# Instance norm on one core: ten middle units loaded in 64 KB rows into pairs of slots, each stored in two column halves

## The chip, the cores and the metric

The kernel runs on one NeuronCore of a Trainium2 chip. A core has a matrix engine (TensorE, PE in the profile), a vector engine (VectorE, DVE), an activation engine (ScalarE, ACT), a general engine (GpSimd, POOL) and SyncE (SP), which here only issues transfers. Sixteen DMA engines, shared by everything the core transfers, carry data between HBM and the on-chip memory of 128 partitions. A transfer issued by SP goes into the ring that the profile calls q1, one issued by ACT into q10, one issued by POOL into q0; each of the sixteen DMA engines has its own piece of each ring.

The metric is device time in microseconds, median over runs. Before the change it is 626.96 us (three runs, 626.79 to 627.2).

## The reference

```python
# x: (4, 8, 16, 256, 256) float32, gamma: (8, 16) float32
mu = x.mean(axis=(3, 4), keepdims=True)
var = ((x - mu) ** 2).mean(axis=(3, 4), keepdims=True)
x_norm = (x - mu) / np.sqrt(var + 1e-5)
out = x_norm * gamma[None, :, :, None, None]
```

There are 4 x 8 x 16 = 512 channels of 65,536 values. Each is normalized by its own mean and variance and multiplied by its gamma (128 different ones). Input and output are 134.2 MB each, and each value is read once and written once.

## The kernel before

**Units.** The 512 channels are cut into 32 units of 16 channels. A channel is spread over S = 8 partitions, 8,192 values (32 KB) in each, so that a unit is a tile of 128 partitions x 8,192 float32 (4 MB), contiguous in HBM. Six such tiles (`slots`, named xt in the profile) hold the units in flight; unit u lives in slot u mod 6.

**One unit.** Its load is issued by SP (L48; units 1 and 3 by ACT). VectorE sums each partition row (L107) while ScalarE squares and sums it (L108), writing the squares to a tile that nobody reads. TensorE multiplies the two columns of sums by a block matrix of -1/65536 (`navg`, L116), which adds up the eight partitions of each channel and hands the negative mean and the negative mean square back to all eight. A chain of small steps on VectorE and ScalarE makes the factor gamma/std (L117 to L127). VectorE then rewrites the tile in place, (x - mean) * scale (L130), and ACT issues its store (L134). At the end of the unit's turn SP is given the load of unit u + 6 (L136), which waits until the store of unit u has landed, since it writes into the same slot.

**Order.** The schedule is written by hand (`manual_schedule`): every engine runs its instructions in the program's order. ACT's queue holds, for each unit, the squares, the root and the issue of the store; the squares of unit u + 1 stand behind the issue of store u, which waits for L130. SP's queue holds only loads, in order.

**Setup.** A 0.5 KB load of gamma goes through POOL (L55). VectorE copies it out eight times (`g_rep`, L83), eight small matmuls turn it into one column per unit of a batch (L88), and a copy brings the columns on chip (`g_col`, L94). POOL builds `navg` (L67 to L72). Ahead of it all, a store of sixteen rows of 512 B of zeros goes to the place of unit 0's output (`touch`, L53 and L54; unit 0's own store overwrites it later and waits for it). The source also has sixty `nop` instructions on ScalarE (L60), which the order of the built program's instructions does not show.

Of the kernel before, what the change touches and what calls it, by code (L numbers as in the profile page):

```python
# [1 line left out]

# [4 lines left out]

F32 = mybir.dt.float32
U8 = mybir.dt.uint8
ALU = mybir.AluOpType  # L10
ACTF = mybir.ActivationFunctionType
AX = mybir.AxisListType


@with_exitstack
def kernel(
    ctx: ExitStack,
    tc: tile.TileContext,
    x: bass.AP,
    gamma: bass.AP,  # L20
    out: bass.AP,
):
    nc = tc.nc
    B, G, C, H, W = x.shape
    P = nc.NUM_PARTITIONS
    HW = H * W
    n_ch = B * G * C
    S = 8
    K = P // S
    F = HW // S  # L30
    U = n_ch // K
    NG = (G * C) // K
    AHEAD = 6
    assert HW % S == 0 and (G * C) % K == 0

    xv = x.rearrange("b g c h w -> (b g c h w)").rearrange("(u p f) -> u p f", p=P, f=F)
    ov = out.rearrange("b g c h w -> (b g c h w)").rearrange("(u p f) -> u p f", p=P, f=F)
    gv = gamma.rearrange("g c -> (g c)")

    data = ctx.enter_context(tc.tile_pool(name="data", bufs=1))  # L40
    singles = ctx.enter_context(tc.tile_pool(name="singles", bufs=1))
    psum = ctx.enter_context(tc.tile_pool(name="psum", bufs=4, space=bass.MemoryType.PSUM))
    ctx.enter_context(tc.manual_schedule())

    slots = [data.tile([P, F], F32, name=f"xt{i}") for i in range(AHEAD)]

    def load(u, queue):
        queue.dma_start(out=slots[u % AHEAD][:], in_=xv[u])  # L48


    g_row = singles.tile([1, G * C], F32, name="g_row")
    touch = singles.tile([16, 128], F32, name="touch")
    nc.vector.memset(touch[:], 0.0)  # L53
    nc.gpsimd.dma_start(out=ov[0][0::S, 0:128], in_=touch[:])  # L54
    nc.gpsimd.dma_start(out=g_row[:], in_=gv[None, :])  # L55
    for u in range(AHEAD):
        load(u, nc.scalar if u in (1, 3) else nc.sync)

    for _ in range(60):
        nc.scalar.nop()  # L60

    eps_t = singles.tile([P, 1], F32, name="eps_t")
    nc.gpsimd.memset(eps_t[:], 1e-5)
    one = singles.tile([1, 1], F32, name="one")
    nc.gpsimd.memset(one[:], 1.0)
    navg = singles.tile([P, K, S], F32, name="navg")
    nc.gpsimd.memset(navg[:], -1.0 / HW)  # L67
    nc.gpsimd.affine_select(  # L68
        out=navg[:], in_=navg[:], pattern=[[-S, K], [0, S]], compare_op=ALU.is_ge,
        fill=0.0, base=0, channel_multiplier=1,  # L70
    )
    nc.gpsimd.affine_select(  # L72
        out=navg[:], in_=navg[:], pattern=[[S, K], [0, S]], compare_op=ALU.is_ge,
        fill=0.0, base=S - 1, channel_multiplier=-1,
    )
    navg_w = navg[:].rearrange("p k s -> p (k s)")
    root_eps = singles.tile([P, 1], F32, name="root_eps")
    nc.scalar.activation(out=root_eps[:], in_=eps_t[:], func=ACTF.Sqrt)  # L78
    g_rep = singles.tile([1, NG, K, S], F32, name="g_rep")
    g_ps = psum.tile([P, NG], F32, name="g_ps", bufs=1)  # L80
    g_col = singles.tile([P, NG], F32, name="g_col")

    nc.vector.tensor_copy(  # L83
        out=g_rep[:],
        in_=g_row[:].rearrange("o (n k) -> o n k", n=NG).unsqueeze(3).to_broadcast([1, NG, K, S]),
    )
    for n in range(NG):
        nc.tensor.matmul(  # L88
            out=g_ps[:, n : n + 1],
            lhsT=g_rep[:, n].rearrange("o k s -> o (k s)"),  # L90
            rhs=one[:],
            start=True, stop=True,
        )
    nc.vector.tensor_copy(out=g_col[:], in_=g_ps[:])  # L94

    junk = singles.tile([P, F], U8, name="junk")

    st = singles.tile([P, U, 2], F32, name="st")
    nvar = singles.tile([P, U], F32, name="nvar")
    std = singles.tile([P, U], F32, name="std")  # L100
    rstd = singles.tile([P, U], F32, name="rstd")
    scale = singles.tile([P, U], F32, name="scale")

    squares = []
    for u in range(U):
        t = slots[u % AHEAD]
        nc.vector.reduce_sum(out=st[:, u, 0:1], in_=t[:], axis=AX.X)  # L107
        square = nc.scalar.activation(  # L108
            out=junk[:], in_=t[:], func=ACTF.Square, accum_out=st[:, u, 1:2],
        )  # L110
        if u:

            tc.declare_no_dep(square.ins, squares[-1].ins, reason="junk, ordered by the root between")
        squares.append(square)
        ps = psum.tile([P, 2], F32, name="ps")
        nc.tensor.matmul(out=ps[:], lhsT=navg_w, rhs=st[:, u], start=True, stop=True)  # L116
        nc.vector.tensor_scalar(  # L117
            out=nvar[:, u : u + 1], in0=ps[:, 0:1], scalar1=ps[:, 0:1],
            scalar2=ps[:, 1:2], op0=ALU.mult, op1=ALU.add,
        )  # L120
        nc.scalar.activation(  # L121
            out=std[:, u : u + 1], in_=nvar[:, u : u + 1], func=ACTF.Sqrt,
            bias=eps_t[:], scale=-1.0,
        )
        nc.vector.reciprocal(out=rstd[:, u : u + 1], in_=std[:, u : u + 1])  # L125
        g = u % NG
        nc.vector.tensor_mul(  # L127
            out=scale[:, u : u + 1], in0=rstd[:, u : u + 1], in1=g_col[:, g : g + 1],
        )
        nc.vector.tensor_scalar(  # L130
            out=t[:], in0=t[:], scalar1=ps[:, 0:1], scalar2=scale[:, u : u + 1],
            op0=ALU.add, op1=ALU.mult,
        )
        nc.scalar.dma_start(out=ov[u], in_=t[:])  # L134
        if u + AHEAD < U:
            load(u + AHEAD, nc.sync)  # L136


# [1 line left out]
_INS = ['x', 'gamma']  # L140
_OUTS = [((4, 8, 16, 256, 256), 'float32')]


# [23 lines left out]
```

## Time and profile before

| | |
|---|---|
| median of three runs | 626.96 us |
| profiled execution, first to last instruction | 624.9 us |
| HBM read and written | 134.22 MB and 134.23 MB |
| VectorE busy | 443.4 us (71%) |
| ScalarE busy | 238.8 us (38%) |
| TensorE, matmuls | 21.4 us (3%) |
| stores, ACT ring, issue to landing | 62.5 us median of 32 |
| loads, SP ring, issue to landing | 38.5 us median of 30 |

The profile's page gives the span of one profiled execution; what lies outside the span is the difference to the measured time. A transfer is cut into packets, one for each row here, and each packet is carried by one DMA engine. The trace records each packet's start, length and size, and this document uses these records beside the page. In the records a packet of 32,768 B takes 1,213 ns, one of 512 B takes 27 ns, and the 4 B packets with which each DMA engine reports the end of its share of a transfer take 9 ns.

### The profile page before, as it was taken

The page shows a single profiled execution, that of the slowest core. Times are in us where ns is not written, and L with a number is a line of the kernel's source. Part 1 is how long each engine was busy: PE and PEld are TensorE (multiplying, and loading weights), DVE is VectorE, ACT ScalarE, POOL GpSimd, SP SyncE. Part 2 cuts the span into 40 slices and gives each one's busy share as a digit, 9 for nine tenths or more (in the row PEclk, how much of TensorE's full clock was granted, in tenths as well). Part 3 has the DMA queues.
Part 4 walks back from the last instruction along what each step waited for, and adds up shares of the span by engine and source line. Part 5 has one row for each costly group of instructions (what it writes and reads, how often), then busy time and mean ns, then how long its engine had stood idle before and what let it go on. Part 6 is the DMA issues. An engine that isn't in the chain of part 4 may idle for free.

```text
span 624.9 us, 631 instructions
## 1 busy us (share of the span) xinstructions
PE 21.4 (3%) x80; PEld 19.5 (3%) x80; DVE 443.4 (71%) x163; ACT 238.8 (38%) x98; POOL 2.4 (0%) x11
## 2 busy tenths in 40 slices
PE   0200000000000000000000000000000000000000
PEld 0200000000000000000000000000000000000000
DVE  0588999999776687666786767867668676687730
ACT  0444444444443234432344423444224442244400
POOL 1000000000000000000000000000000000000000
DMA  8999999999999999999999999999999999999998
GB/s 370 436 426 430 422 434 436 436 436 437 432 424 433 436 436 424 436 436 434 436 436 432 422 436 436 434 426 436 436 434 436 436 434 419 436 436 434 426 436 369
DMA packets 9282, 268.46 MB, mean 430 GB/s; under 512 B 1072, under 2 KB 1088, under 8 KB 1088
## 3 DMA queue, kind: packets, MB, share of 16 engines
q10 hardware_dynamic: 4896, 142.61, 52.9%
q1 hardware_dynamic: 4320, 125.83, 46.8%
q0 software_dynamic: 64, 0.01, 0.0%
q14 instruction: 2, 0.02, 0.0%
HBM read 134.22 MB, written 134.23 MB: 430 GB/s over the span
## 4 chain that ended last, share of the span: by engine, by line
another core or an unknown queue 61%; DMA 17%; DVE 15%; SPq 1%; PE 1%; issue 0%; ACT 0%
DVE st L107 10%; DMA xt<-in_x_dram 10%; DMA out_dram<-xt 8%; DVE xt L130 5%; SPq L48 1%; PE ps L116 1%; ACT std L121 0%; DVE nvar L117 0%; DVE rstd L125 0%; DVE scale L127 0%
## 5 line engine op out<-in xcount | busy, mean ns | idle before, releaser
L107 DVE TENSOR_REDUCE st<-xt 128x1 f32<-128x8192 f32 x32 | 277.9, 8685 | 100.4 <-DMA xt<-in_x_dram 100.4
L108 ACT ACTIVATE junk<-xt 128x8192 uint8<-128x8192 f32 x32 | 225.0, 7030 | 275.1 <-DMA xt<-in_x_dram 231.9
L130 DVE TENSOR_SCALAR xt<-xt,ps,scale 128x8192 f32<-128x8192 f32 x32 | 145.6, 4550 | 1.2
L121 ACT ACTIVATE std<-nvar,eps_t 128x1 f32<-128x1 f32 x32 | 9.4, 294 | 79.6 <-DVE nvar L117 79.6
L116 PE MATMUL ps<-st,navg 128*128 128x2 f32 x64 | 17.9, 349 | 557.1 <-DVE st L107 557.1
L116 PEld LDWEIGHTS ps<-st,navg 128*128 128x128 f32 x64 | 16.0, 311 | 558.9 <-issue 558.9
L117 DVE TENSOR_SCALAR nvar<-ps 128x1 f32<-128x1 f32 x32 | 9.2, 287 | 23.8 <-PE ps L116 23.8
L125 DVE RECIPROCAL rstd<-std 128x1 f32<-128x1 f32 x32 | 5.2, 164 | 11.6 <-ACT std L121 11.6
L83 DVE COPY g_rep<-g_row 1x1024 f32<-1x1024 f32 x1 | 0.7, 681 | 14.3 <-DMA g_row<-in_gamma_dram 14.3
L108 ACT ACTIVATION_READ_ACCUMULATOR junk<-xt 128x1 f32 x32 | 6.0, 186 | 0.0
L127 DVE TENSOR_TENSOR scale<-rstd,g_col 128x1 f32<-128x1 f32 x32 | 5.1, 159 | 1.1
L88 PE MATMUL g_ps<-one,g_rep 1*128 1x1 f32 x16 | 3.5, 347 | 16.1 <-DVE g_rep L83 16.1
L88 PEld LDWEIGHTS g_ps<-one,g_rep 1*128 1x128 f32 x16 | 3.5, 325 | 16.1 <-issue 16.1
L94 DVE COPY g_col<-g_ps 128x8 f32<-128x8 f32 x1 | 0.2, 166 | 3.7 <-PE g_ps L88 3.7
L78 ACT ACT_TABLE_LOAD x1 | 1.3, 1283 | 1.7 <-PEq L151 1.7
L53 DVE MEMSET touch<- 16x128 f32 x1 | 0.2, 165 | 0.9 <-PEq L151 0.9
L54 POOL DMA_DIRECT2D out_dram<-touch x1 | 0.6, 619 | 0.8 <-DVE touch L53 0.8
L55 POOL DMA_DIRECT2D g_row<-in_gamma_dram x1 | 0.5, 487 | 0.0
L68 POOL TENSOR_SCALAR_AFFINE_SELECT navg<-navg 128x128 f32<-128x128 f32 x1 | 0.4, 400 | 0.1
L72 POOL TENSOR_SCALAR_AFFINE_SELECT navg<-navg 128x128 f32<-128x128 f32 x1 | 0.4, 399 | 0.1
L67 POOL MEMSET navg<- 128x128 f32 x1 | 0.2, 232 | 0.0
L78 ACT ACTIVATE root_eps<-eps_t 128x1 f32<-128x1 f32 x1 | 0.2, 203 | 0.0
(6 smaller groups left out, 0.6 us busy)
## 6 DMA issues: line engine op xcount, KB each, us to landing
out_dram<-xt ACTq DMA_DIRECT2D x32, 4096.0 KB, 62.5
xt<-in_x_dram SPq DMA_DIRECT2D x30, 4096.0 KB, 38.5
xt<-in_x_dram ACTq DMA_DIRECT2D x2, 4096.0 KB, 31.5
out_dram<-touch POOLq DMA_DIRECT2D x1, 8.0 KB, 9.1
g_row<-in_gamma_dram POOLq DMA_DIRECT2D x1, 0.5 KB, 13.3
```

What stands on the lines that cost most here:

```text
L48: queue.dma_start(out=slots[u % AHEAD][:], in_=xv[u])
L78: nc.scalar.activation(out=root_eps[:], in_=eps_t[:], func=ACTF.Sqrt)
L83: nc.vector.tensor_copy(out=g_rep[:], in_=g_row[:].rearrange("o (n k) -> o n k", n=NG).unsqueeze(3).to_broadcast([1, NG, K, S]),)
L88: nc.tensor.matmul(out=g_ps[:, n : n + 1], lhsT=g_rep[:, n].rearrange("o k s -> o (k s)"), rhs=one[:], start=True, stop=True,)
L107: nc.vector.reduce_sum(out=st[:, u, 0:1], in_=t[:], axis=AX.X)
L108: square = nc.scalar.activation(out=junk[:], in_=t[:], func=ACTF.Square, accum_out=st[:, u, 1:2],)
L116: nc.tensor.matmul(out=ps[:], lhsT=navg_w, rhs=st[:, u], start=True, stop=True)
L117: nc.vector.tensor_scalar(out=nvar[:, u : u + 1], in0=ps[:, 0:1], scalar1=ps[:, 0:1], scalar2=ps[:, 1:2], op0=ALU.mult, op1=ALU.add,)
L121: nc.scalar.activation(out=std[:, u : u + 1], in_=nvar[:, u : u + 1], func=ACTF.Sqrt, bias=eps_t[:], scale=-1.0,)
L125: nc.vector.reciprocal(out=rstd[:, u : u + 1], in_=std[:, u : u + 1])
L127: nc.vector.tensor_mul(out=scale[:, u : u + 1], in0=rstd[:, u : u + 1], in1=g_col[:, g : g + 1],)
L130: nc.vector.tensor_scalar(out=t[:], in0=t[:], scalar1=ps[:, 0:1], scalar2=scale[:, u : u + 1], op0=ALU.add, op1=ALU.mult,)
```

## The change

Units 0 to 5 and 26 to 31 of before stay as they are (narrow units). The twenty between them become ten wide units of 32 channels. A wide unit's channel lies in 4 partitions, 16,384 values (64 KB) in each, and the unit fills a pair of neighbouring slots, seen as 128 partitions x 16,384. The six slots are now three such pairs. In the order of the loop there are 22 units: 6 narrow, 10 wide, 6 narrow.

A wide unit is loaded by one transfer of 128 rows of 64 KB, when both slots of its pair are free. The sums, the squares and the rewrite are each done in two column halves of 8,192; two matmuls, one for each half, add into the same result; the small chain runs once for the unit. Each half has its own store, of 128 rows of 32 KB that lie 64 KB apart in HBM. The loads' order is worked out ahead: `behind[u]` lists the loads that stand in SP's queue after unit u.

The setup makes `navg` and the gamma columns twice, once for each width, through one shared buffer `g_all`. The `touch` store and the `nop` instructions are gone.

```diff
-    slots = [data.tile([P, F], F32, name=f"xt{i}") for i in range(AHEAD)]
+    pairs = [data.tile([P, 2, F], F32, name=f"xt{i}") for i in range(SLOTS // 2)]
+    while at < total:
+        wide = 2 if ENDS <= at < total - ENDS else 1
+        units.append((at, wide, slot))
+        at += wide
+        slot = (slot + wide) % SLOTS
...
     def load(u, queue):
-        queue.dma_start(out=slots[u % AHEAD][:], in_=xv[u])
+        queue.dma_start(out=on_chip(u), in_=in_dram(xf, u))
...
+    for u in range(U):
+        free += held[u]
+        while nxt < U and held[nxt] <= free:
+            free -= held[nxt]
+            behind[u].append(nxt)
+            nxt += 1
...
-    touch = singles.tile([16, 128], F32, name="touch")
-    nc.vector.memset(touch[:], 0.0)
-    nc.gpsimd.dma_start(out=ov[0][0::S, 0:128], in_=touch[:])
...
-    for _ in range(60):
-        nc.scalar.nop()
...
+    for wide in (1, 2):
+        s = S // wide
+        k = K * wide
+        ng = GC // k
...
+        g_rep = g_all[:, : GC * s].rearrange("o (n k s) -> o n k s", n=ng, k=k)
...
-        nc.vector.reduce_sum(out=st[:, u, 0:1], in_=t[:], axis=AX.X)
-        square = nc.scalar.activation(
-            out=junk[:], in_=t[:], func=ACTF.Square, accum_out=st[:, u, 1:2],
-        )
...
-        nc.tensor.matmul(out=ps[:], lhsT=navg_w, rhs=st[:, u], start=True, stop=True)
+        for h in range(wide):
+            part = t[:, h * F : (h + 1) * F]
+            nc.vector.reduce_sum(out=st[:, u, 2 * h : 2 * h + 1], in_=part, axis=AX.X)
+            square = nc.scalar.activation(
+                out=junk[:], in_=part, func=ACTF.Square, accum_out=st[:, u, 2 * h + 1 : 2 * h + 2],
+            )
...
+            nc.tensor.matmul(
+                out=ps[:], lhsT=navg[wide], rhs=st[:, u, 2 * h : 2 * h + 2],
+                start=h == 0, stop=h == wide - 1,
+            )
...
-        nc.scalar.dma_start(out=ov[u], in_=t[:])
-        if u + AHEAD < U:
-            load(u + AHEAD, nc.sync)
+        for h in range(wide):
+            part = t[:, h * F : (h + 1) * F]
+            nc.vector.tensor_scalar(
+                out=part, in0=part, scalar1=ps[:, 0:1], scalar2=scale[:, u : u + 1],
+                op0=ALU.add, op1=ALU.mult,
+            )
+            nc.scalar.dma_start(out=in_dram(of, u)[:, h * F : (h + 1) * F], in_=part)
+        for v in behind[u]:
+            load(v, nc.sync)
```

## The prediction

> **What bounds the kernel now.** I read the page's slices and packet rows first, then stretches of the middle, SyncE's own waits, and the two ends in order of time.
>
> ```profile
> span 624.9 us, 631 instructions
> PE 21.4 (3%) x80; PEld 19.5 (3%) x80; DVE 443.4 (71%) x163; ACT 238.8 (38%) x98; POOL 2.4 (0%) x11
> ...
> DMA  8999999999999999999999999999999999999998
> ...
> DMA packets 9282, 268.46 MB, mean 430 GB/s; under 512 B 1072, under 2 KB 1088, under 8 KB 1088
> ...
> q10 hardware_dynamic: 4896, 142.61, 52.9%
> q1 hardware_dynamic: 4320, 125.83, 46.8%
> ...
> L107 DVE TENSOR_REDUCE st<-xt 128x1 f32<-128x8192 f32 x32 | 277.9, 8685 | 100.4 <-DMA xt<-in_x_dram 100.4
> ...
> L130 DVE TENSOR_SCALAR xt<-xt,ps,scale 128x8192 f32<-128x8192 f32 x32 | 145.6, 4550 | 1.2
> ```
>
> The two rings fill 52.9 + 46.8 = 99.7% of sixteen DMA engines' span, in every slice. No compute engine is near that.
>
> ```profile
> 178.90:198.30 19.40, 0.56 (x2) 0.50 (x2) 13.91 (x6) 7.48 (x4) 0.00 (x0) 1.00 1.00 432
> 430.50:449.90 19.40, 0.56 (x2) 0.50 (x2) 13.88 (x6) 7.45 (x4) 0.00 (x0) 1.00 1.00 432
> ```
>
> ```profile
> SPq L48 <- DMA out_dram<-xt: 534.4, 26, 59.5
> ```
>
> In the middle a unit takes 19.36 us (the chain of waits has SyncE's loads at 178.96, 198.30, 217.66). In the stretches above, VectorE is busy 13.9 us of it (fifth column), DMA all of it (next to last). SyncE waits 534.4 us for stores to land, yet no DMA engine idles, since the rings hold other work. So the time is packets: each engine carries 8,192 / 16 = 512 data packets.
>
> **The packet price.** The trace's packet records give 1,213 ns for 32,768 B and 27 ns for 512 B, so 1,186 ns for 32,256 B: 0.03677 ns a byte. 32,768 B at that rate are 1,204.8 ns; 8.2 ns are fixed. In the records a packet starts 4 ns before the one ahead of it ends, so 4.2 ns of the fixed part count, and a 9 ns report counts 5. Check: 16 data packets at 1,209 ns and 2 reports make 19.354 us a unit, against 19.36.
>
> **The change, part by part.**
>
> *Wide loads.* Ten loads of 128 rows of 64 KB take the place of twenty of 128 rows of 32 KB: per DMA engine 80 packets fewer. I price each at the 4.2 ns from the records: -0.34 us. Bounds: 0, if a row is still carried as two packets, and the whole fixed part, 80 x 8.2 = -0.66. No row shows a packet over 32 KB; a loss has to be bounded too, below. Ten reports fewer per engine: 10 x 5 ns = -0.05. Stores keep 32 KB rows and add none.
>
> *The touch store.* Its packets go: 27 + 9 - 8 = 0.03 us per engine. What else it may do: the records show the first real stores (39.8 us) with 118 ns over the usual price per engine on average, and the load packets behind them (41.3 us) with 524 ns, together 0.64 us, with the touch present. Without it, this may come once more: +0.64. But the touch's own packets, the first writes of the run, took 27 ns each and nothing beside them was slow, so I take -0.03. The nops are in neither the trace nor the built program: ScalarE's table load starts at 1.72 us, 0.04 after its second issue ended. Zero.
>
> *Setup twice.* Hidden behind the first load:
>
> ```profile
> 15.32 0.68 DVE L83 COPY g_rep<-g_row 1x1024 f32<-1x1024 f32 x1 [14.27 <-DMA g_row<-in_gamma_dram]
> 16.12 3.48 PEld L88 LDWEIGHTS g_ps<-one,g_rep 1*128 1x128 f32 x16 [16.12 <-issue]
> 16.15 3.54 PE L88 MATMUL g_ps<-one,g_rep 1*128 1x1 f32 x16 [16.15 <-DVE g_rep L83]
> 19.73 0.17 DVE L94 COPY g_col<-g_ps 128x8 f32<-128x8 f32 x1 [3.72 <-PE g_ps L88]
> 22.62 7.03 ACT L108 ACTIVATE junk<-xt 128x8192 uint8<-128x8192 f32 x1 [19.41 <-DMA xt<-in_x_dram]
> 22.62 8.69 DVE L107 TENSOR_REDUCE st<-xt 128x1 f32<-128x8192 f32 x1 [2.73 <-DMA xt<-in_x_dram]
> ```
>
> The second set begins at 19.90, since it shares the buffer: half a copy 0.34, a handover 0.12, half the matmuls 1.77, the copy back 0.2, so 22.3, before the first load lands at 22.6. Were the cover gone, VectorE's early chain would shift by 2.5 us, which the next part affords.
>
> *Coarser grain, new waits.* A wide load waits for two stores, and SyncE's later loads queue behind it. Would both rings run empty? A wide unit's latency on VectorE is 2 x 8.69 + 1.78 (31.32 to 33.10, sums to rewrite, in the chain of waits) + 2 x 4.55 = 28.3 us, in a period of 2 x 19.36 = 38.7; the first half is stored after 23.7. Rings are dry only if all three pairs sit between landing and their first store; with 10.4 us to spare per unit VectorE has at most one. The two transitions need their own sums:
>
> Start: six narrow loads (58.1 us of packets from 1.8) alternate with stores issued at 37.7, 52.6 and 67.5, VectorE's pace of 14.93. By about 79 the rings have carried six loads and two stores (77.4); store 1 lands, and the first wide load sends its first packet 1.5 us later (landing to SyncE about 0.5, issue to first packet 1.0, as from 0.80 to 1.80 at the start). Store 2, issued at 67.5, still has over 8 us of packets. Margin 7 us. The next two wide loads wait for stores 3 and 5 while the stores after them are queued or a wide load is running.
>
> End:
>
> ```profile
> 585.26 8.69 DVE L107 TENSOR_REDUCE st<-xt 128x1 f32<-128x8192 f32 x1 [4.35 <-DMA xt<-in_x_dram]
> ...
> 600.32 0.34 ACTq L134 DMA_DIRECT2D out_dram<-xt  x1
> ```
>
> The last store is issued 22.4 us before the packets end (622.7), and needs 9.7 of them: 11.7 us to spare. Worked forward packet by packet in these durations, before has the last load landing at 581 (it was 585.2) and after at 573, with no idle time in either: the margin at the end grows. In the same working 12 us more on VectorE per wide unit bring the first gap.
>
> Here a rule speaks against the change. In the records q1 and q10 alternate packet by packet. The Trainium skill, "DMA: Bandwidth & Descriptors", section "Queues, rings and completion order", states that each DMA engine takes turns between rings at packet granularity; the trace agrees, with every q1 packet followed by one of q10 once both are filled. With 64 KB load packets, loads then get two thirds while both rings are filled; by it, stores would land later and slots come free later.
>
> *That as a sum.* A wide load beside stores lands after 8 x (2.41 + 1.21) = 29 us, and for the remaining 9.7 of 38.7 stores run alone. Total work is the same, so without a dry ring it costs 0.
>
> **Sum.** -0.34 - 0.05 - 0.03 = -0.42 us. The profiled execution: 624.91 to 624.5 of span; with the 2.05 around it (626.96 - 624.91), 626.5.
>
> **Rivals.**
>
> *Rows still carried as two packets* (the change doesn't do what it says): -0.08, 626.9. Nothing in before tells it.
>
> *The wide rows themselves are slower.* Something in 64 KB packets, or in rows 64 KB apart, keeps a DMA engine from its steady rate. For: the records have 31 store packets between 50 and 75 us that took 52 ns more each, so a store's packet can be slowed. Against: past 100 us nearly all take 1,213. With 52 ns on each of 80 wide packets, 626.9 + 4.2 = 631.1; at half of that 629.0. It makes the kernel slower by over 1.25 us from 21 ns a packet ((1.25 + 0.42) / 80). [...]
>
> *A ring dry at the first wide load.* If store 2 were done before it arrives, each such gap costs the 1.5 us handover; at the start and three times more that is 6 us, 632.5. It decides from 7 us of delay. Against: the sums above.
>
> *The touch held off more than the rows show*, over 1.7 us: 628.5. Only the slow packets at 41 us speak for it.
>
> *Faster by over 0.2%:* the fixed part gone whole (-0.66), reports (-0.09) and the 0.64 at 40 us gone too: -1.39, 625.6. It needs all three at once.
>
> **Chances.** Forecast (with its touch bound, up to 627.2) 0.62, two packets 0.08, slower rows 0.16, dry ring 0.06, touch 0.03, faster 0.05. A measurement of this kernel tells about 0.2%, 1.25 us, from no change: faster 0.05, same 0.70, slower 0.25. The likeliest's own range is 626.1 to 627.2. The range goes down to the faster case, 625.7, and up to half the slow-row price, 629.0; left out are the upper half of slow rows, the dry ring and a part of the faster case, 0.17.
>
> **What would show it.** Records of 64 KB packets at 2,418 ns and 9282 - 1280 - 160 - 32 = 7810 packets on the page; two 32 KB ones instead name the first rival, over 2,439 ns the second. Nines in every DMA slice but the ends, SyncE's wide loads 38.7 us apart, loads landing 30 us after issue. A slice under 9 near 80 us or in the middle names the dry ring; slow packets at 40 us the touch. Wrong altogether: a time with DMA full in every slice and packets at these prices that is still over 1.25 us off.

## The result, and the profile after

The changed kernel takes 628.74 us (median of six runs, 627.65 to 629.12), the kernel before 626.81 us beside it (six runs, 626.71 to 627.2). The ratio is 1.0026, with a 95% interval of 1.0015 to 1.0038: slower, by 0.15 to 0.38%. The forecast was 626.5 and no change that a measurement can tell. The time lies in the stated range, 625.7 to 629.0, but on the slower side, which had a quarter of the chance.

The page of the changed kernel, its first rows, transfers and issues:

```profile
span 627.0 us, 588 instructions
...
DMA  8999999999999999999999999999999999999997
GB/s 372 433 424 431 433 395 445 420 452 418 449 416 433 446 414 433 431 448 422 433 458 418 449 418 424 435 464 406 460 406 435 433 433 435 433 435 435 433 432 341
DMA packets 7811, 268.47 MB, mean 428 GB/s; under 512 B 896, under 2 KB 896, under 8 KB 896
...
q10 hardware_dynamic: 4896, 142.61, 52.8%
q1 hardware_dynamic: 2880, 125.83, 46.7%
q8 instruction: 1, 0.02, 0.0%
...
L154 DVE TENSOR_REDUCE st<-xt 128x1 f32<-128x8192 f32 x32 | 277.0, 8681 | 120.1 <-DMA xt<-in_x_dram 120.1
...
L180 DVE TENSOR_SCALAR xt<-xt,ps,scale 128x8192 f32<-128x8192 f32 x32 | 144.7, 4549 | 0.8
...
out_dram<-xt ACTq DMA_DIRECT2D x32, 4096.0 KB, 46.3
xt<-in_x_dram SPq DMA_DIRECT2D x10, 4096.0 KB, 28.4
...
xt<-in_x_dram SPq DMA_DIRECT2D x10, 33.1
```

Most of the forecast's signs are there: 7,811 packets against a forecast of 7,810 (the one more is the fetch of instructions in q8), and DMA nines in every slice but the ends. Wide loads land 33.1 us after their issue, where 30 was forecast. The sixth slice of GB/s (78 to 94 us) has 395, the lowest but for the ends: the engines are busy there with packets that take longer. The wide loads keep their pace of 38.7 us, as the chain of waits shows (start, length, what):

```profile
200.34 0.33 SPq L71
200.66 38.36 another core or an unknown queue
...
239.10 0.33 SPq L71
```

Stretches of 20 us around the first wide load, of the kernel before and then of the changed one (last column GB/s, next to last the DMA share):

```profile
60.00:80.00 20.00, 1.12 (x4) 1.01 (x4) 17.64 (x10) 7.84 (x6) 0.00 (x0) 1.00 1.02 437
80.00:100.00 20.00, 0.56 (x2) 0.50 (x2) 18.82 (x7) 9.62 (x4) 0.00 (x0) 1.00 1.00 433
```

```profile
60.00:80.00 20.00, 1.11 (x4) 1.00 (x4) 17.65 (x10) 7.95 (x6) 0.00 (x0) 1.00 1.03 446
80.00:100.00 20.00, 0.56 (x2) 0.50 (x2) 18.82 (x7) 9.52 (x4) 0.00 (x0) 1.00 1.01 408
```

The share of busy time is the same, with 408 GB/s against 433. This alone is a hint and no measure: a stretch counts the packets that start in it, and one packet of 32 KB more or less on every engine is 26 GB/s over 20 us.

The issue of load 6 in the kernel before, and of the first wide load in the changed one (start, length, what):

```profile
62.36 0.33 SPq L48 DMA_DIRECT2D xt<-in_x_dram  x1
```

```profile
81.74 0.33 SPq L71 DMA_DIRECT2D xt<-in_x_dram  x1
```

The packet records say which packets. In the changed kernel the load ring q1 has nothing from 79.9 us, when the last narrow load's packets end, to 86.0: the first wide load is issued at 81.74, after store 1 has landed. In the kernel before load 6 is issued at 62.36, behind store 0 alone, and its packets follow those of load 5 without a gap. In the changed kernel, from 84.7 us all sixteen engines carry a slow store packet (up to 1,845 ns in place of 1,213), and then the first wide packets take 2,952 to 4,152 ns. One engine also stands idle for 0.78 us at 87.7, ahead of its first wide packet, although store packets are waiting. A few more packets are slow until 93 us. Of the 1,280 packets of 64 KB in the run, 1,238 take 2,418 ns to within 2 ns, which is the price that was forecast.

The table has one profiled execution of each kernel, the later rows from the experiments below. It sums, for one DMA engine (a sixteenth of the total), what packets took beyond their usual 1,213 or 2,418 ns, in microseconds; stretches are in us from the span's start. The last columns are when the engines' last data packet ends. The records do not name the engine of a packet; here each packet is put to the engine whose packet ended as it began.

```text
kernel                 0-20   35-64  64-110  110-135  135-280  280-310  310-end | mean    slowest
before                 0.49   0.71   0.05    0.00     0.06     0.00     0.01    | 623.07  623.60
changed                0.50   0.75   1.44    0.01     0.15     0.01     0.13    | 624.41  625.64
touch put back         0.58   0.91   1.04    0.02     0.08     0.07     0.24    | 624.26  625.67
halves, late           0.52   0.78   1.52    0.00     0.05     0.00     0.05    | 624.76  625.71
halves, early          0.64   0.85   0.00    0.00     0.16     0.00     0.06    | 623.36  624.39
before, dry at 80      0.65   0.70   1.66    0.00     0.05     0.00     0.03    | 624.76  625.83
first wide early       0.59   0.93   0.00    1.30     0.10     0.01     0.13    | 624.44  626.11
before, dry at 274     0.57   0.82   0.00    0.01     0.15     0.59     0.06    | 623.91  625.75
before, dry twice      0.51   0.85   1.19    0.00     0.05     0.00     0.03    | 624.47  625.20
restart beside loads   0.58   1.14   0.00    0.00     0.07     0.01     0.04    | 623.52  624.42
changed, that start    0.73   0.83   0.05    0.01     0.32     0.04     0.30    | 623.61  624.43
that start, no hold    0.57   1.06   0.00    0.00     0.06     0.00     0.04    | 623.48  624.18
```

The second row against the first is the answer to where the time went. The engines end 1.34 us later on average: -0.42 by the forecast's packet terms, +1.39 in the stretch around 86 us, +0.22 after 110 us, +0.05 before 64, and 0.05 and 0.06 for the idle 0.78 us and the 0.94 us of the instruction fetch, each on one engine of sixteen. The slowest engine ends 2.04 us later. The slow packets fall unevenly, 0.95 to 2.23 us an engine in the stretch around 86 us, the slowest engine is the one with the idle 0.78 us, and the kernel ends with its slowest. The spans differ by 2.1 us, the medians by 1.93.

### The profile page after: what moved, and what is told of

Its sections match the earlier page's. It is cut to its first block, busy times and chain, and to the rows that moved or that the text cites. A ratio compares the mean times of both kernels' runs of the same rounds, so it can differ in the third digit from the quotient of the medians.

```text
span 627.0 us, 588 instructions
## 1 busy us (share of the span) xinstructions
PE 23.2 (4%) x88; PEld 21.3 (3%) x88; DVE 435.9 (70%) x134; ACT 235.9 (38%) x88; POOL 3.1 (0%) x13
## 2 busy tenths in 40 slices
DMA packets 7811, 268.47 MB, mean 428 GB/s; under 512 B 896, under 2 KB 896, under 8 KB 896
## 4 chain that ended last, share of the span: by engine, by line
another core or an unknown queue 40%; DMA 33%; DVE 20%; PE 1%; issue 0%; ACT 0%; SPq 0%
DMA xt<-in_x_dram 18%; DMA out_dram<-xt 15%; DVE st L154 14%; DVE xt L180 6%; PE ps L161 1%; ACT std L169 0%; DVE nvar L165 0%; SPq L71 0%; DVE rstd L173 0%; DVE scale L175 0%
## 5 line engine op out<-in xcount | busy, mean ns | idle before, releaser
L169 ACT ACTIVATE std<-nvar,eps_t 128x1 f32<-128x1 f32 x22 | 6.5, 295 | 68.7 <-DVE nvar L165 68.7
L165 DVE TENSOR_SCALAR nvar<-ps 128x1 f32<-128x1 f32 x22 | 6.3, 287 | 16.4 <-PE ps L161 16.4
L173 DVE RECIPROCAL rstd<-std 128x1 f32<-128x1 f32 x22 | 3.6, 164 | 8.0 <-ACT std L169 8.0
L125 DVE COPY g_all<-g_row 1x1024 f32<-1x1024 f32 (+1 forms) x2 | 1.1, 542 | 10.6 <-DMA g_row<-in_gamma_dram 10.6
L130 PE MATMUL g_ps<-one,g_all 1*128 1x1 f32 x24 | 5.4, 348 | 12.0 <-DVE g_all L125 12.0
L130 PEld LDWEIGHTS g_ps<-one,g_all 1*128 1x128 f32 x24 | 5.3, 324 | 12.1 <-issue 11.4
L175 DVE TENSOR_TENSOR scale<-rstd,g_col 128x1 f32<-128x1 f32 x22 | 3.5, 159 | 0.7
## 6 DMA issues: line engine op xcount, KB each, us to landing
xt<-in_x_dram SPq DMA_DIRECT2D x10, 33.1
```

The costliest lines, as they stand in the source:

```text
L125: nc.vector.tensor_copy(out=g_rep, in_=g_row[:].rearrange("o (n k) -> o n k", n=ng).unsqueeze(3).to_broadcast([1, ng, k, s]),)
L130: nc.tensor.matmul(out=g_ps[:, n : n + 1], lhsT=g_rep[:, n].rearrange("o k s -> o (k s)"), rhs=one[:], start=True, stop=True,)
L165: nc.vector.tensor_scalar(out=nvar[:, u : u + 1], in0=ps[:, 0:1], scalar1=ps[:, 0:1], scalar2=ps[:, 1:2], op0=ALU.mult, op1=ALU.add,)
L169: nc.scalar.activation(out=std[:, u : u + 1], in_=nvar[:, u : u + 1], func=ACTF.Sqrt, bias=eps_t[:], scale=-1.0,)
L175: nc.vector.tensor_mul(out=scale[:, u : u + 1], in0=rstd[:, u : u + 1], in1=g_cols[wide][:, g : g + 1],)
```

## The experiments

The theory at the outset, **D**: the load ring running dry and restarting beside stores makes packets slow. Its first rivals: **W**, that the first 64 KB packets are slow as such, and **T**, the missing touch store.

**The touch store put back.**

```diff
+    touch = singles.tile([16, 128], F32, name="touch")
+    nc.vector.memset(touch[:], 0.0)
+    nc.gpsimd.dma_start(out=in_dram(of, 0)[0::S, 0:128], in_=touch[:])
     nc.gpsimd.dma_start(out=g_row[:], in_=gv[None, :])
```

> The changed kernel with the touch store put back. Theory D (the load ring runs dry at 80.6 us and its restart at 86 us beside stores costs 1.4 us a DMA engine, more on the slowest): the touch is no part of it, 628.7 us, slow packets at 85 to 92 us as in the changed kernel. Theory W (the first packets of 64 KB are slow because they are 64 KB): the same. Rival T (the touch was what held the loss off): 627.2 or less, and the slow packets at 85 us gone.

Measured 629.09 us, ratio to the kernel before 1.0036 (1.0023 to 1.0048). The slow packets near 86 us are there (third row). T falls: the touch neither held them off nor made the packets around 40 us faster (0.91 with it, 0.75 without). The slowest engine's end in this row is not the restart's alone: it carries the instruction fetch of 0.94 us at 593 us, and the next engine ends 0.77 us earlier.

**Wide loads as two loads of 32 KB rows, second half first.**

```diff
-        queue.dma_start(out=on_chip(u), in_=in_dram(xf, u))
+        if units[u][1] == 1:
+            queue.dma_start(out=on_chip(u), in_=in_dram(xf, u))
+            return
+        for h in (1, 0):
+            cols = slice(h * F, (h + 1) * F)
+            queue.dma_start(out=on_chip(u)[:, cols], in_=in_dram(xf, u)[:, cols])
```

> The changed kernel, each wide load issued as two loads of 32 KB rows, the second column half first, so that the load ring still runs dry until store 1 has landed (first wide packet near 86 us). Theory D: slow packets at 85 to 92 us stay, some 1 to 1.5 us a DMA engine, and the time is 628.3 to 629.2. Theory W: no 64 KB packet, so no slow packets there, 626.5 to 627.1.

Measured 629.27 us, 1.0033 (1.0021 to 1.0046). There is no 64 KB packet, and the loss is whole: 1.52 us an engine, first wide packet at 86.4. W falls.

**The same, first half first** (`for h in (0, 1)`).

> The same two loads of 32 KB rows, first column half first: it waits for store 0 alone and is issued near 62 us, so the load ring does not run dry at 80. Theory D: no slow packets at 85 us, 626.5 to 627.1. Theory W: 626.5 to 627.1 too. A third cause (two column halves, one unit of 32 channels, rows 64 KB apart) would leave it at 628.5 or above.

Measured 627.45 us, 1.0008 (0.9999 to 1.0017). The first half's load is issued at 62.4, the ring stays filled, and no packet between 64 and 135 us is slow. The two last kernels differ in the order of the two issues of each wide unit alone. The median is a little above the range that was given, and the interval takes in no change. The third cause falls too, since all its parts are in this kernel.

**The kernel before, dry once at 80 us.** The smallest form of the change's wait, without wide units:

```diff
-        if u + AHEAD < U:
+        if u == 1:
+            load(7, nc.sync)
+            load(6, nc.sync)
+        elif u and u + AHEAD < U:
             load(u + AHEAD, nc.sync)
```

> The kernel before, with only this edit: load 7 stands ahead of load 6 in SyncE's queue, so that both wait for store 1 and the load ring runs dry once, at 80 us, with 32 KB rows that are contiguous. Theory D: slow packets at 85 to 90 us and 628.0 to 628.8. Theory W: nothing, 626.6 to 627.0.

Measured 629.14 us, 1.0035 (1.0022 to 1.0047). Two issues swapped in the old kernel cost as much as the whole change. Its page and its stretch from 80 us:

```profile
DMA  9999999999999999999999999999999999999998
GB/s 370 435 431 426 431 408 416 435 433 426 431 435 424 435 435 435 435 435 435 431 435 435 431 435 435 435 435 433 435 433 435 431 428 435 435 424 435 435 435 353
```

```profile
80.00:100.00 20.00, 0.56 (x2) 0.50 (x2) 18.83 (x7) 9.62 (x4) 0.00 (x0) 1.00 1.00 398
```

The DMA row is full and the sixth and seventh slices carry 408 and 416 in place of 435. Here the slow packets come in two groups: mostly store packets at 84.8 to 86.1, and at 94.3 to 96.3 the load's fourth and fifth packets on the engines. D is shown for the stretch near 80 us.

Next, why the changed kernel's nine later restarts are cheap although its ring runs dry ahead of each wide load, for about 10 us: **F**, only the first restart is dear, wherever it comes; **S**, only the stretch near 80 us is.

**Only the first wide unit as two early halves.**

```diff
-        queue.dma_start(out=on_chip(u), in_=in_dram(xf, u))
+        if u != ENDS:
+            queue.dma_start(out=on_chip(u), in_=in_dram(xf, u))
+            return
+        for h in (0, 1):
+            cols = slice(h * F, (h + 1) * F)
+            queue.dma_start(out=on_chip(u)[:, cols], in_=in_dram(xf, u)[:, cols])
```

> The changed kernel with only the first wide unit loaded as two loads of 32 KB rows, first half first, so that the load ring stays filled at 80 us; the other nine wide loads keep their 64 KB rows, and the ring first runs dry near 117 us, to restart near 125. Theory F (the first restart of the load ring is dear wherever it comes, the later ones cheap): the slow packets move from 85 to about 125 us, 1 to 1.5 us a DMA engine, 628.3 to 629.2. Theory S (only a dry ring in the stretch near 80 us is dear): no slow packets at 80 to 130 us, and 626.3 to 627.2.

Measured 629.18 us, 1.0031 (1.002 to 1.0042). The loss moved with the restart. Stretches from 80, 120 and 160 us:

```profile
80.00:100.00 20.00, 0.56 (x2) 0.50 (x2) 18.82 (x7) 9.66 (x4) 0.00 (x0) 1.00 0.98 421
120.00:140.00 20.00, 1.12 (x4) 1.01 (x4) 18.82 (x7) 7.42 (x3) 0.00 (x0) 1.00 1.00 406
160.00:180.00 20.00, 1.12 (x4) 1.00 (x4) 18.82 (x7) 10.49 (x5) 0.00 (x0) 1.00 1.06 457
```

Again single rates swing by a packet an engine; the records have no slow packet from 64 to 110 us and 1.30 us an engine from 110 to 135, nearly all of it at 124 to 131.

**The kernel before, dry once in the middle.**

```diff
-        if u + AHEAD < U:
+        if u == 12:
+            load(18, nc.sync)
+            load(16, nc.sync)
+            load(17, nc.sync)
+        elif u not in (10, 11) and u + AHEAD < U:
             load(u + AHEAD, nc.sync)
```

> The kernel before, 32 KB rows throughout, with loads 16 and 17 held behind load 18 in SyncE's queue, so that the load ring runs dry once, in the middle, from about 215 us until the restart near 235 us, beside stores. Theory F: slow packets at that restart, 1 to 1.5 us a DMA engine, 628.3 to 629.2. Theory S: none, 626.8 to 627.4.

Measured 628.43 us, 1.0036 (1.0015 to 1.0057). The ring was dry from 274 to 288.8 us, later than stated, because loads already queued reach further than I had counted. The stretch of the restart cost 0.59 us an engine, less than was expected, most of it at 299 to 306 us. The slowest engine ended 2.15 us after that of the kernel before, and 0.80 us of that is a pause of this engine alone at 300.8. The times scatter more here: four of the eleven runs took 627.67 to 627.82, three 630.49 to 634.64. S falls by the median and by the slow packets, but the cost of a restart in the middle is less sure than that of one at 80 us.

**The kernel before, dry twice** (both edits above in one).

> The kernel before with the load ring run dry twice: at 80 us (load 7 ahead of load 6) and again near 275 us (load 18 ahead of loads 16 and 17), 32 KB rows throughout. Theory F (only the first restart is dear): slow packets at 86, 1 to 1.6 us a DMA engine, and under 0.2 us at the restart near 287; 628.5 to 629.5. Rival (each restart of 32 KB rows is dear, and the changed kernel's later ones are cheap for another reason): 0.5 us or more a DMA engine at both, 629.5 to 631.

Measured 628.93 us, 1.0038 (1.0023 to 1.0052). 1.19 us an engine at the first restart and nothing at the second, at 290 us, where a first one had cost 0.59. F stands for this start of the kernel.

**An early restart beside loads.** If the first restart is dear because it is SP's ring's first (**R**), an earlier one would take it over; if it is the first time that loads begin beside lone stores (**M**), it would not.

```diff
-    for u in range(AHEAD):
-        load(u, nc.scalar if u in (1, 3) else nc.sync)
+    for u in range(AHEAD - 1):
+        load(u, nc.sync if u == 0 else nc.scalar)
...
         nc.vector.reduce_sum(out=st[:, u, 0:1], in_=t[:], axis=AX.X)
+        if u == 0:
+            nc.vector.memset(slots[5][:, 0:1], 0.0)
+            load(5, nc.sync)
...
-        if u + AHEAD < U:
+        if u == 1:
+            load(7, nc.sync)
+            load(6, nc.sync)
+        elif u and u + AHEAD < U:
             load(u + AHEAD, nc.sync)
```

> The kernel before with units 1 to 4 loaded through ACT's ring, load 5 held on SP until VectorE has summed unit 0 (near 32 us, by a memset of one column of its slot, which its load overwrites), and loads 7 and 6 behind store 1: SP's ring runs dry at about 22 us and restarts near 33 us beside loads alone, and again at about 85 us beside stores. Theory R (a ring's own first restart is dear): slow packets near 33 us, none at 85. Theory M (what is dear is the first time that loads begin beside stores that run alone): nothing much near 33 us, 1 to 1.6 us a DMA engine at 85, 628.5 to 629.5.

Measured 627.19 us, 1.0003 (0.9993 to 1.0012). Neither: no slow packet at the restart at 35 us and none at 85.7 us. In this start four loads stand ahead of the first store in ACT's ring. The first store packet comes at 61.5 us (at 43.0 in the kernel before), when SP's ring has been dry since 52.5, so that the stores begin alone. The stretch from 35 to 64 us costs more here (1.14 us, against 0.71 to 0.93); the slow packets in it are the last two load packets of ACT's ring on the engines, at 58.0 to 60.3.

**That start in the changed kernel** (the first two parts of the last edit), which also asks whether the early restart was the cause.

> The changed kernel with the start of the last experiment: units 1 to 4 through ACT's ring, load 5 held on SP until VectorE has summed unit 0, so that SP's ring restarts once near 35 us beside loads. The wide loads keep their 64 KB rows, and the ring still runs dry ahead of each. Theory F' (the first restart of SP's ring is dear only beside stores; one beside loads is cheap and spares all later ones): no slow packets near 85 us, 626.4 to 627.3, the price of 64 KB rows alone. Rival (it was not the early restart that spared it): slow packets near 85 us and 628.3 to 629.3.

Measured 627.85 us, 1.0014 (1.0005 to 1.0024). The slow packets near 86 us are gone but for one, and with them most of the loss; the time is still above the stated range. Its table row has 0.66 us an engine after 135 us (0.32 + 0.04 + 0.30), most of it at the later restarts: dry rings are not quite free there, and eat the 0.42 us that the fewer packets save. One of the eleven runs took 629.51.

**That start in the kernel before, without the hold.**

```diff
     for u in range(AHEAD):
-        load(u, nc.scalar if u in (1, 3) else nc.sync)
+        load(u, nc.sync if u in (0, 5) else nc.scalar)
...
-        if u + AHEAD < U:
+        if u == 1:
+            load(7, nc.sync)
+            load(6, nc.sync)
+        elif u and u + AHEAD < U:
             load(u + AHEAD, nc.sync)
```

> The kernel before with units 1 to 4 through ACT's ring and loads 7 and 6 behind store 1, as in the experiment with the early restart, but load 5 issued at once: SP's ring carries units 0 and 5 without a gap, runs dry near 41 us and restarts for the first time near 85 us beside stores. Theory F': 1 to 1.6 us a DMA engine of slow packets near 85 us, 628.3 to 629.3. Rival (the units on ACT's ring, not the early restart, spared it): none near 85, 627.0 to 627.5.

Measured 627.29 us, 1.0004 (0.9996 to 1.0013). There is no early restart, the ring is dry from 40.5 to 85.7 us, and the restart is free all the same in the profiled execution (one of the eleven runs took 629.41):

```profile
80.00:100.00 20.00, 0.56 (x2) 0.50 (x2) 18.82 (x7) 9.54 (x4) 0.00 (x0) 1.00 0.99 429
```

The records have no slow packet from 64 to 110 us. So it was not the early restart that spared it; the way the six loads are shared between the rings did, or what follows from it.

**What stays open.** Why that start spares the restart. Three ideas fall to the records at hand. The engines are equally in step ahead of a dear restart and a free one (their progress differs by 0.53 us in the old kernel made dry at 80, by 0.62 in the last kernel). Stores alone are not dear: the kernel before ends on 39 us of them, and no packet there is more than 41 ns over its price. And loads that begin beside lone stores are not dear as such, by the last three kernels. That the dear restart needs stores that had first begun beside loads fits all twelve kernels and was not tried by itself. Other things that go with this start fit as well, such as SP's ring having carried two loads instead of four or more.

## Why the prediction was wrong

- **The bound** was right: sixteen busy DMA engines, and the time is in the main the sum of their packets.
- **The packet price** was right: 2,418 ns for 64 KB to the nanosecond, 7,811 packets. The -0.42 us closes the account of the engines' ends above; it is too small for a measured time to have shown it alone.
- **The setup and the transitions** were right in the main: both rings are never dry together, and the tail has time to spare. The figures differ. The second gamma columns were done at 17.6 us, not 22.3, since gamma's load landed at 10.6 instead of 14.3; with the touch put back they were done at 22.3. The last load landed at 583.1, not 573 (585.3 in the kernel before), and the last store was issued 26.2 us before the engines' average end (22.8 in the kernel before). The margin of before had been given as 11.7 us, and its own terms, 22.4 less 9.7, make 12.7.
- **The step that failed** is "Total work is the same, so without a dry ring it costs 0", with "Rings are dry only if all three pairs sit between landing and their first store". It counted a ring's emptiness only where both are empty and an engine stops. The wait on two stores (first wide load issued at 81.74 against 62.36) empties the load ring alone; the engines stay busy with stores, and the restart then makes packets slow on all sixteen. It cost 1.44 us an engine, and the old kernel with two issues swapped shows it (1.66) without any other part of the change. Why the restart slows packets stays open: with four of the first loads in ACT's ring a ring just as dry restarts free, so the dry ring is needed and not enough.
- **The slowest engine**: the sum was made for an average engine. The slowest lost 0.70 us more than the average (2.04 - 1.34), by uneven slow packets and one pause of 0.78 us, for which the prediction had no term.
- **The rivals**: "dry ring" had the place, 80 us, but the wrong mechanism, a gap of 1.5 us after 7 us of delay. The first wide packet came at 86.0 instead of about 80.5, within that margin, and store packets filled the time. "The wide rows are slower" had its sign, packets over 2,439 ns, mainly at the first restart; it falls with the kernels that lose the same on 32 KB rows, and store packets of rows 64 KB apart take 1,213 ns in the middle like the others. "Touch" falls to its own experiment. The bound of 0.64 us for it was not used, and rested on a misreading: the slow packets at 39.8 us are the last load packets of ACT's ring, and the first store packet comes at 43.0.
- **The range**: its upper end was half the price of slower rows, added to 626.9. Added to the forecast's 626.5 the price gives 630.7, and half of it 628.6, just short of the measured 628.74. That the time lies in the range is luck: the upper end stood for a cause that was not at work.
- **The restart's delay**: 1.0 us from issue to first packet was taken from the quiet start; at the restarts beside stores it was 3.4 to 4.8 us.

## What to carry to other kernels

When DMA is the bound, a full row of nines is not proof of full speed: read GB/s beside it, and the lengths of single packets where it dips. Before a coarser transfer is made to wait for two releases, ask not only whether the engines run idle but whether one ring does while the other runs; splitting every wide transfer, so that its first half goes at the first release, removed the loss here (627.45, against 629.27 with the second half first). Splitting only the first one moved the loss to the next restart (629.18). And weigh it against what is to be had: at 4.2 ns a packet, and with the reports and the touch, there was 0.42 us to gain in 627.

## What the hardware showed that was not expected

- A load ring that restarts beside stores sends its first packet 3.4 to 4.8 us after the issue, and beside loads 3.7 us, against 1.0 us at the start with nothing running. The Trainium skill, "DMA: Bandwidth & Descriptors", section "Latency and other measured facts", states about 600 ns to the first byte; the start took 0.4 us more than that, the restarts several times as long.
- The first such restart slows packets of both rings for some microseconds (0.6 to 1.7 us an engine in seven kernels), later ones hardly (0.00 to 0.1 us), and with four of the first loads in ACT's ring not even the first. The slow packets begin ahead of the restarted ring's first packet: in the changed kernel at 84.7 us, on store packets, where the first wide packet comes at 86.0.
- One DMA engine fetches 16 KB of instructions (q8 in the page). In the changed kernel this is a packet of 0.94 us at 596 us, inside the span, on one engine that ends among the last, and in its five variants one of 0.88 to 0.94 us at 593 to 604 us. In the kernel before it comes at 625 us, after the last store, and so it does in that kernel's variants.
